# Output projection: high and low activations side by side, 512 columns in one product and 64 in a second

## The chip, the cores and the metric

The kernel runs on one core of a Trainium2 chip. Its time is the device time of one execution in microseconds (us), here the median of the runs shown. The profile of one execution, taken by the hardware, gives the busy time of each engine, every instruction's start and length, and the chain of work that ended last. The engines are TensorE (PE; its weight loads are listed apart as PEld), VectorE (DVE), ScalarE (ACT), GpSimd (POOL) and SyncE (SP), which issues most transfers.

## What is computed

One layer of a decoder for two groups of requests that share their weights: 256 prompt tokens and 8 x 4 sample tokens, 288 tokens together, each of width 4096. The change touches the last matrix product and what follows it:

```
merged = sigmoid(g_a) * (attn @ w_pa) + sigmoid(g_b) * (out_b @ w_pb)
y = merged @ w_o
x = layer_norm(ALPHA * x + gate[:, None] * y, ln_g, ln_b)
```

`w_o` is 4096 x 4096, all data fp32.

## The kernel before

Everything is kept with features on the 128 partitions and the 288 tokens along the row (`T = 288`), so a tile of activations is 128 x 288 and a block of weights 128 x 128. Weights come from memory in units of 128 x 2048 (1 MB, 16 blocks), loaded on SP's queue two units ahead. Each operand is split into a high part (the value cast to fp32r) and a low part (what the cast left out). ScalarE casts half a unit, 8 blocks, to `wH` (line 181), VectorE subtracts to get `wL` (line 182); there are three buffers of either (`HB = 3`). A product of two split operands is then three products in the array, all added up in one PSUM tile (`prod`, lines 190 to 195):

- line 193: `wH` with the high activations,
- line 194: `wH` with the low activations,
- line 195: `wL` with the high activations.

Stages run one after another over one stream of weight units: the modulation and the first column tiles of the input projection (`ada`, `ea`), the other column tiles with attention and gating in the background (`in`), the two merge projections (`p`), and the output projection (`y`). The merge (lines 717 to 743) leaves `merged` split into `mH` and `mL`, two tiles of 16 feature blocks each. The output projection (`o_units`, from line 763) makes 32 tiles of 128 features: 32 blocks of weights for each, in two units, 96 products into one PSUM tile `y` of 128 x 288 out of three such. `post_o` (line 801) then reads `y` from PSUM: the gate is multiplied in and `ALPHA * x` added (lines 805 to 808, VectorE), ScalarE squares (line 815), VectorE adds up sums and squares (lines 820, 821), ScalarE multiplies by the gain (line 824). After the first tile a product with ones (`kp`, line 811) gives a mean that is subtracted from all later tiles. `token_sums` (line 795) sums over features for the norm, and `final` spreads the statistics and writes the result.

Instructions are written in the order of the program and then put in an order for each engine by a scheduler that works with estimates; each engine runs its own list in order. In PSUM there are three tiles with the tag `acc`, four with the tag `bg` for the background work, and one for the modulation.

Of the kernel before, what the change touches and what calls it, by code (L numbers as in the profile page):

```python
# [10 lines left out]
F32 = mybir.dt.float32  # L11
F32R = mybir.dt.float32r
# [6 lines left out]
P = 128  # L19
D = 4096  # L20
KT = D // P
# [52 lines left out]
def first_order(au, eu, extra):  # L74
    """Order of the units of the modulation (au) and of the column tiles summed up as h comes (eu): per unit
    of column tiles, RATIO units of the modulation in the first half of h and RATIO2 in the second, where
    the extra tiles, which need the first half only, fill in. Returns the order and what is left."""
    order = []
    ada = [(c, u) for c, us in enumerate(au) for u in us]
    early = [(c, u) for c, us in enumerate(eu) for u in us]  # L80
    extra = list(extra)
    credit, at, go = 0.0, -1, False
    half = OFFS.index(KT // 2)
    while ada:
        at = ada[0][0]
        ratio = RATIO if at < half else RATIO2
        ready = early and early[0][0] < at
        if ready and at < half and early[0][0] == at - 1 and sum(1 for x in early if x[0] == at - 1) <= RES:
            ready = False
        if credit < 1.0:  # L90
            go = False
        elif credit >= (GE if at < half else GE2):
            go = True
        if go and ready:
            order.append(early.pop(0)[1])
            credit -= 1.0
        elif go and at >= half and extra:
            order.append(extra.pop(0))
            credit -= 1.0
        else:  # L100
            order.append(ada.pop(0)[1])
            credit = min(credit + 1.0 / ratio, CAP + 1.0 / ratio + (GE if at < half else GE2) - 1.0)
    return order, extra[:4] + [u for _, u in early] + extra[4:]
# [6 lines left out]
def build(ctx, tc, nc, I, O):  # L110
# [16 lines left out]

    # constants
    ident = const.tile([P, P], F32, name="ident")
# [16 lines left out]

    # background work: generators stepped between the weight units
    bg = []
# [15 lines left out]

    # weight units
    class Unit:
# [45 lines left out]

# [1 line left out]
    ada_row = [0]  # L214

    # Column group q of the array takes a quarter of the unit's columns; where a chunk has too few of
    # them, groups 0 and 1 take the shift and scale of even rows of weights, 2 and 3 those of odd ones.
    def ada_units(n, fin):
# [100 lines left out]

# [1 line left out]
    Q = slot("Q")  # L321
# [65 lines left out]

# [1 line left out]
    def attn_setup():  # L389
# [51 lines left out]
    def softmax_tail(m, sm, sk, ex, r):  # L441
        # m: the negated maxima; sm: sums without the sink; r: reciprocal of the whole sum
        nc.vector.tensor_tensor(ex, sk, m, ALU.add)
        nc.scalar.activation(ex, ex, AF.Exp)
        nc.vector.tensor_tensor(sm, sm, ex, ALU.add)
        nc.vector.reciprocal(r, sm)

    def attn_group(g):
# [6 lines left out]

        # heads in the order (half, pair), so that each bank is written from one half of the partitions
        def q(half, i, a, b):
            return Q[64 * half:64 * half + 64, 4 * g + i, a:b]
        # scores
        pss = [bgp("s0") for _ in range(2)]  # L460
# [8 lines left out]
        for ih in range(2):  # L469
# [10 lines left out]
            yield 1800  # L480
        # softmax
        st = A["st"].rearrange("p (a n h) -> p a n h", a=4, n=2)
# [14 lines left out]
        for hb in range(2):  # L497
# [5 lines left out]
            yield 1000  # L503
        # sample scores
        Qbd, Qs, Ss = A["Qbd"], A["Qs"], A["Ss"]
        for b in range(NB):
# [4 lines left out]
                                  Q[:, 4 * g:4 * g + 4, NPR + TS * b:NPR + TS * b + TS])  # L511
        # transposes
        for i in range(6):
# [9 lines left out]
        for hf in range(2):  # L523
# [8 lines left out]
            yield 1800  # L532
        # prompt outputs
        for qi in range(4):
# [8 lines left out]
            yield 1300  # L543
        # sample softmax
        m, sm, ex, r = (A["st"][:, 32 + 2 * i:34 + 2 * i] for i in range(4))
# [27 lines left out]

# [1 line left out]
    G = {}  # L575
# [137 lines left out]

# [1 line left out]
    M = {}  # L715

    def p_units(j):
        def load(k):
            t = tmp.tile([P, T], F32, tag="t", name="gl", bufs=6)
            nc.sync.dma_start(t, gdram[32 * k + j])  # L720
            nc.scalar.activation(t, t, AF.Sigmoid)
            return t

        def body_for(name, k):
            def body(u):
                if j == 0 and k == 1:
                    M["H"] = [slot(f"mH{i}", dt=F32R) for i in range(2)]
                    M["L"] = [slot(f"mL{i}", dt=F32R) for i in range(2)]
                t = load(k)
                ps = acc("p")  # L730
                for i in range(16):
                    prod(ps, u, i, G[name + "H"][:, i], G[name + "L"][:, i], i == 0, i == 15)
                nc.vector.tensor_mul(t, t, ps)
                if k == 0:
                    M[j] = t
                else:
                    ta = M.pop(j)
                    nc.vector.tensor_add(t, t, ta)
                    h, lo = M["H"][j // 16][:, j % 16], M["L"][j // 16][:, j % 16]
                    nc.scalar.copy(h, t)  # L740
                    nc.vector.tensor_sub(lo, t, h.bitcast(F32))
            return body
        return [Unit(I["wpa"][j], body_for("A", 0)), Unit(I["wpb"][j], body_for("B", 1))]

# [1 line left out]
    Z = {}  # L746

    def start_final():
        w = slot("fin", (P, 4608))
        cut = lambda i: w[:, P + i * T:P + (i + 1) * T]  # L750
        Z["ones"] = w[:, :P]
        for i, n in enumerate(("K", "s1", "s2", "dg", "dg2", "rstd", "row", "w")):
            Z[n] = cut(i)
        Z["dg"] = w[:, P + 3 * T:P + 5 * T]
        nc.vector.memset(Z["ones"], 1.0)
        nc.vector.memset(Z["row"][0:2], 1.0)
        Z["d"] = [slot(f"d{i}") for i in range(2)]
        Z["gb"] = slot("gb", (P, 4608))[0:2, :D]
        nc.scalar.dma_start(Z["gb"], I["gbrow"])
        # the table of the last square root, ahead of its use  # L760
        nc.scalar.activation(Z["w"][:, 0:1], epst, AF.Sqrt)

    def o_units(j):
        st = {}

        def body_for(half):
            def body(u):
                if half == 0:
                    st["ps"] = acc("y")
                    st["x"] = tmp.tile([P, T], F32, tag="t", name="xl", bufs=6)  # L770
                    nc.sync.dma_start(st["x"], I["xT"][:, j])
                elif j == 0:
                    nc.scalar.mul(st["x"], st["x"], ALPHA)
                else:
                    if j == 1 or j == KT - 1:
                        drain()
                    nc.vector.scalar_tensor_tensor(st["x"], st["x"], ALPHA, Z["K"], ALU.mult, ALU.subtract)
                    if j == KT - 1:
                        Z["st"] = bgp("st")
                        Z["st2"] = bgp("st2")  # L780
                for i in range(16):
                    if half and j == KT - 1 and i == 8:
                        token_sums(Z["s1"], Z["s2"], True)
                    prod(st["ps"], u, i, M["H"][half][:, i], M["L"][half][:, i], half == 0 and i == 0,
                         half == 1 and i == 15)
                if half == 1:
                    post_o(j, st["ps"], st["x"])
            return body
# [11 lines left out]
    def post_o(j, ps, x):  # L800
        # d = ALPHA * x + gate * y - K; K is the mean over the first 128 features, for every token
        z = Z["d"][j // 16][:, j % 16]
# [23 lines left out]
    def final():  # L826
        # the tokens on partitions (3 blocks of TB) for their statistics
        sums = Z["w"][:TB, 18:24]
# [10 lines left out]
        nc.vector.tensor_mul(r2[:, :, 1], mean, r2[:, :, 0])  # L839
        # and spread over all partitions: rstd and -mean * rstd  # L840
        dg = Z["dg"][:TB].rearrange("p (s b t) -> p s b t", s=2, b=3)
# [9 lines left out]

        # out = (d * gain) * rstd + (gain * nmr + bias)
        def tiles(j):
# [23 lines left out]

        # shared out between VectorE and GpSimd; the second term from ScalarE or TensorE
        clock, done = {"g": 0.0, "v": 0.0}, []
# [7 lines left out]

# [1 line left out]
    items = []  # L889
# [127 lines left out]
```

## Time and profile before

| what | value |
|---|---|
| median of two runs (3073.05 and 3073.66) | 3073.36 us |
| span of the profiled execution, first to last instruction | 3070.7 us |
| what the runs shown have beyond that span | 2.7 us by the median (2.3 to 3.0) |
| products of the input projection, `ea` and `in` | 5376 and 8832 |
| products of the merge, `p` | 3072 |
| products of the output projection, `y` | 3072 |
| weight units of the output projection | 64, 1 MB each, 4.9 us from issue to landing |
| first and last product of `y` | at 2630.4 and 3041.5 us |

The profile lists no other time for the profiled execution than its span. "Busy" of TensorE counts a product from its start to its modelled end, and products overlap, so the rate is read from the distance of two starts. In the rows of a group stand the line, the engine, the operation, output and inputs by their names in the program, the tile of the array (rows x columns), the shape, the count, then the busy time, the mean length in ns and the idle time before them.

### The profile page before, as it was taken

The page shows a single profiled execution, that of the slowest core. Times are in us where ns is not written, and L with a number is a line of the kernel's source. Part 1 is how long each engine was busy: PE and PEld are TensorE (multiplying, and loading weights), DVE is VectorE, ACT ScalarE, POOL GpSimd, SP SyncE. Part 2 cuts the span into 40 slices and gives each one's busy share as a digit, 9 for nine tenths or more (in the row PEclk, how much of TensorE's full clock was granted, in tenths as well). Part 3 has the DMA queues.
Part 4 walks back from the last instruction along what each step waited for, and adds up shares of the span by engine and source line. Part 5 has one row for each costly group of instructions (what it writes and reads, how often), then busy time and mean ns, then how long its engine had stood idle before and what let it go on. Part 6 is the DMA issues. An engine that isn't in the chain of part 4 may idle for free.

```text
span 3070.7 us, 53243 instructions
## 1 busy us (share of the span) xinstructions
PE 3036.1 (99%) x23040; PEld 2843.1 (93%) x23040; DVE 1550.5 (50%) x2202; ACT 1080.1 (35%) x1381; POOL 15.4 (1%) x14
## 2 busy tenths in 40 slices
PE   7999999999999999999999999999999999999998
PEld 5888888888999999999999999999999999999997
DVE  3776554444445545445444633444555555555555
ACT  2222223322333434343333333333444444433333
POOL 0000000000000000000000000000000000000001
PEclk8999999999999999999999999999999999999998
DMA  8888877877777565555655565566565555555552
GB/s 333 326 335 327 326 287 297 304 279 285 259 256 262 178 221 209 185 209 205 215 206 206 206 213 200 209 222 215 203 212 188 188 188 188 175 176 177 177 177 95
DMA packets 128383, 700.07 MB, mean 228 GB/s; under 512 B 14802, under 2 KB 44530, under 8 KB 48882
## 3 DMA queue, kind: packets, MB, share of 16 engines
q1 hardware_dynamic: 109440, 669.56, 60.8%
q10 hardware_dynamic: 18708, 27.10, 2.5%
q8 instruction: 181, 2.97, 0.4%
q14 instruction: 54, 0.44, 0.0%
HBM read 676.85 MB, written 19.46 MB: 227 GB/s over the span
## 4 chain that ended last, share of the span: by engine, by line
PE 98%; DMA 1%; DVE 1%; issue 0%; ACT 0%; ACTq 0%; DVEq 0%; SPq 0%
PE in L193 13%; PE in L195 13%; PE in L194 13%; PE ea L193 8%; PE ea L194 8%; PE ea L195 8%; PE ada L233 6%; PE p L193 5%; PE y L193 5%; PE p L195 4%; PE y L195 4%; PE p L194 4%; PE y L194 4%; DMA lngb<-lngb 0%; DMA raw<-wada 0%; PE pT L517 0%
## 5 line engine op out<-in xcount | busy, mean ns | idle before, releaser
L181 ACT CAST wH<-raw 128x1024 fp32r<-128x1024 f32 x848 | 888.8, 1050 | 1841.5 <-PE in L194 813.1
L182 DVE TENSOR_TENSOR wL<-raw,wH 128x1024 fp32r<-128x1024 f32 x848 | 1035.4, 1224 | 973.6 <-ACT wH L181 970.8
L193 PE MATMUL in<-hH,wH 128*128 128x288 f32 x2944 | 883.1, 300 | 0.0
L194 PE MATMUL in<-hL,wH 128*128 128x288 f32 x2944 | 870.5, 296 | 0.0
L195 PE MATMUL in<-hH,wL 128*128 128x288 f32 x2944 | 866.7, 294 | 0.0
L193 PEld LDWEIGHTS in<-hH,wH 128*128 128x128 f32 x2944 | 552.2, 188 | 32.7 <-ACT wH L181 9.2
L195 PEld LDWEIGHTS in<-hH,wL 128*128 128x128 f32 x2944 | 554.7, 188 | 0.0
L194 PEld LDWEIGHTS in<-hL,wH 128*128 128x128 f32 x2944 | 553.1, 188 | 0.1
L193 PE MATMUL ea<-hH,wH 128*128 128x288 f32 x1792 | 537.3, 301 | 2.4 <-ACT hH L297 2.4
L194 PE MATMUL ea<-hL,wH 128*128 128x288 f32 x1792 | 529.8, 296 | 1.4 <-DVE hL L298 1.4
L195 PE MATMUL ea<-hH,wL 128*128 128x288 f32 x1792 | 524.7, 295 | 0.0
L193 PEld LDWEIGHTS ea<-hH,wH 128*128 128x128 f32 x1792 | 336.7, 188 | 52.4 <-ACT wH L181 23.9
L194 PEld LDWEIGHTS ea<-hL,wH 128*128 128x128 f32 x1792 | 337.7, 188 | 1.9 <-DVE hL L298 1.8
L195 PEld LDWEIGHTS ea<-hH,wL 128*128 128x128 f32 x1792 | 337.3, 189 | 1.7 <-issue 0.8
L193 PE MATMUL y<-mH,wH 128*128 128x288 f32 x1024 | 303.4, 296 | 0.0
L194 PE MATMUL y<-mL,wH 128*128 128x288 f32 x1024 | 302.6, 296 | 0.0
L195 PE MATMUL y<-mH,wL 128*128 128x288 f32 x1024 | 301.4, 294 | 0.0
L233 PE MATMUL ada<-raw,cT 128*32 128x512 f32 (+1 forms) x1792 | 202.0, 549 | 16.2 <-ACT cT L136 8.2
L195 PEld LDWEIGHTS y<-mH,wL 128*128 128x128 f32 x1024 | 193.1, 189 | 0.1
L194 PEld LDWEIGHTS y<-mL,wH 128*128 128x128 f32 x1024 | 192.4, 188 | 0.1
L193 PEld LDWEIGHTS y<-mH,wH 128*128 128x128 f32 x1024 | 192.1, 188 | 0.0
L193 PE MATMUL p<-AH,wH 128*128 128x288 f32 x512 | 151.8, 297 | 0.0
(200 smaller groups left out, 2388.7 us busy)
## 6 DMA issues: line engine op xcount, KB each, us to landing
raw<-wada SPq DMA_DIRECT2D x192, 1024.0 KB, 5.2
raw<-wr SPq DMA_DIRECT2D x184, 1024.0 KB, 5.1
raw<-we SPq DMA_DIRECT2D x112, 1024.0 KB, 7.2
raw<-wo SPq DMA_DIRECT2D x64, 1024.0 KB, 4.9
raw<-wpa SPq DMA_DIRECT2D x32, 1024.0 KB, 4.9
raw<-wpb SPq DMA_DIRECT2D x32, 1024.0 KB, 4.9
gl<-gdram SPq DMA_DIRECT2D x64, 144.0 KB, 3.2
pdram<-part ACTq DMA_DIRECT2D x32, 144.0 KB, 4.6
```

What stands on the lines that cost most here:

```text
L181: nc.scalar.copy(h, s)
L182: nc.vector.tensor_sub(lo, s, h.bitcast(F32))
L193: mm(ps, wh, xh, start=first, stop=False)
L194: mm(ps, wh, xl, start=False, stop=False)
L195: mm(ps, wl, xh, start=False, stop=last)
L233: mm(st["ps"][32 * q:32 * q + 32, :w], cT[:, kt, :], u.raw[:, at:at + w], start=kt < 1 + paired, stop=kt >= KT - 1 - paired)
```

## The change

The merge now writes the high and low part of a feature block side by side: four tiles `mHL` of 8 feature blocks, each block 2 x 288 columns. The output projection passes these 576 columns by `wH` in two products, the first 512 and the last 64, into two PSUM tiles; `wL` with the 288 high columns is the third and adds to the first 288 columns of the wide tile. At the end of an output tile the two halves of the sum are put together in SBUF, and `post_o` reads that. The second PSUM tile has the tag `bg`. Nothing else of the program is changed.

```
-                    M["H"] = [slot(f"mH{i}", dt=F32R) for i in range(2)]
-                    M["L"] = [slot(f"mL{i}", dt=F32R) for i in range(2)]
+                    M["HL"] = [slot(f"mHL{i}", (P, 8, 2, T), F32R) for i in range(4)]
...
-                    h, lo = M["H"][j // 16][:, j % 16], M["L"][j // 16][:, j % 16]
+                    h, lo = M["HL"][j // 8][:, j % 8, 0], M["HL"][j // 8][:, j % 8, 1]
...
+    WIDE = 512
+
+    def prod_wide(ps, ps2, unit, m, hl, first, last):
+        pump(PUMP)
+        wh, wl = unit.block(m)
+        flat = hl.rearrange("p s t -> p (s t)")
+        mm(ps, wh, flat[:, :WIDE], start=first, stop=False)
+        mm(ps2[:, :2 * T - WIDE], wh, flat[:, WIDE:], start=first, stop=last)
+        mm(ps[:, :T], wl, hl[:, 0], start=False, stop=last)
...
-                    st["ps"] = acc("y")
+                    st["ps"] = ps_acc.tile([P, WIDE], F32, tag="acc", name="y")
+                    st["ps2"] = bgp("y2")
...
-                    prod(st["ps"], u, i, M["H"][half][:, i], M["L"][half][:, i], half == 0 and i == 0,
-                         half == 1 and i == 15)
+                    k = half * 16 + i
+                    prod_wide(st["ps"], st["ps2"], u, i, M["HL"][k // 8][:, k % 8], k == 0, k == KT - 1)
                 if half == 1:
-                    post_o(j, st["ps"], st["x"])
+                    y = tmp.tile([P, T], F32, tag="t", name="ysum", bufs=6)
+                    n = WIDE - T
+                    nc.scalar.copy(y, st["ps"][:, :T])
+                    nc.vector.tensor_add(y[:, :n], y[:, :n], st["ps"][:, T:])
+                    nc.vector.tensor_add(y[:, n:], y[:, n:], st["ps2"][:, :T - n])
+                    post_o(j, y, st["x"])
```

What this does to the order of the engines' lists. TensorE, end of the first output tile and start of the second, before (the numbers after the names tell buffers apart):

```order
L193 MATMUL y_25537<-mH1_21524,wH_25459 128x288
L194 MATMUL y_25537<-mL1_21526,wH_25459 128x288
L195 MATMUL y_25537<-mH1_21524,wL_25460 128x288
L193 MATMUL y_25670<-mH0_21523,wH_25529 128x288
L194 MATMUL y_25670<-mL0_21525,wH_25529 128x288
L195 MATMUL y_25670<-mH0_21523,wL_25530 128x288
```

And now, with the wide product on line 770, the narrow one on 771 and the third on 772:

```order
L770 MATMUL y_25537<-mHL3_21526,wH_25459 128x512
L771 MATMUL y2_25538<-mHL3_21526,wH_25459 128x64
L772 MATMUL y_25537<-mHL3_21526,wL_25460 128x288
L770 MATMUL y_25675<-mHL0_21523,wH_25529 128x512
L772 MATMUL y_25675<-mHL0_21523,wL_25530 128x288
```

Three products a block as before, of other widths; in the second tile alone the narrow products of the first ten blocks are put off. They follow the product `kp`, which before stood two blocks and a product into the tile:

```order
L195 MATMUL y_25670<-mH0_21523,wL_25530 128x288
L193 MATMUL y_25670<-mH0_21523,wH_25529 128x288
L811 MATMUL kp_25651<-d0_25522,fin_25519 128x288
L194 MATMUL y_25670<-mL0_21525,wH_25529 128x288
L195 MATMUL y_25670<-mH0_21523,wL_25530 128x288
```

TensorE at the same place now, ten blocks into the tile:

```order
L770 MATMUL y_25675<-mHL1_21524,wH_25533 128x512
L772 MATMUL y_25675<-mHL1_21524,wL_25534 128x288
L828 MATMUL kp_25656<-d0_25522,fin_25519 128x288
L771 MATMUL y2_25676<-mHL0_21523,wH_25529 128x64 x8
L771 MATMUL y2_25676<-mHL1_21524,wH_25533 128x64 x2
```

The mean of the first tile is taken eight blocks later than before. From the third tile on the three products of every block stand together.

VectorE at the end of a tile in the middle of the stage, before:

```order
L805 TENSOR_TENSOR t2_26812<-y_26702,gate_82 128x32
L808 SCALAR_TENSOR_TENSOR d0_25522<-y_26702,gate_82,xl_26703 128x256
L807 TENSOR_TENSOR d0_25522<-t2_26812,xl_26703 128x32
L820 TENSOR_TENSOR fin_25519<-fin_25519,d0_25522 128x288
L182 TENSOR_TENSOR wL_26756<-raw_26753,wH_26755 128x1024
L821 TENSOR_TENSOR fin_25519<-fin_25519,sq_26816 128x288
```

VectorE at the same place now:

```order
L802 TENSOR_TENSOR ysum_26858<-ysum_26858,y_26747 128x224
L803 TENSOR_TENSOR ysum_26858<-ysum_26858,y2_26748 128x64
L822 TENSOR_TENSOR t2_26862<-ysum_26858,gate_82 128x32
L825 SCALAR_TENSOR_TENSOR d0_25522<-ysum_26858,gate_82,xl_26749 128x256
L824 TENSOR_TENSOR d0_25522<-t2_26862,xl_26749 128x32
L837 TENSOR_TENSOR fin_25519<-fin_25519,d0_25522 128x288
L838 TENSOR_TENSOR fin_25519<-fin_25519,sq_26866 128x288
L182 TENSOR_TENSOR wL_26806<-raw_26799,wH_26805 128x1024
```

Two adds have come in ahead, and the next `wL` stands behind the sum of squares instead of ahead of it. ScalarE there, before:

```order
L181 CAST wH_26755<-raw_26753 128x1024
L815 ACTIVATE sq_26816<-d0_25522 128x288
L824 ACTIVATE d0_25522<-d0_25522,lngb_81 128x288
L181 CAST wH_26759<-raw_26753 128x1024
L181 CAST wH_26823<-raw_26821 128x1024
```

ScalarE now:

```order
L181 CAST wH_26801<-raw_26799 128x1024
L801 COPY ysum_26858<-y_26747 128x288
L832 ACTIVATE sq_26866<-d0_25522 128x288
L181 CAST wH_26805<-raw_26799 128x1024
L841 ACTIVATE d0_25522<-d0_25522,lngb_81 128x288
L181 CAST wH_26873<-raw_26871 128x1024
```

The copy from PSUM has come in ahead of the square, and the multiplication by the gain stands one cast later.

## The prediction

> **What bounds the kernel now.** I read the page first (shares of the engines, the chain that ended last), then the output projection by windows, then single products.
>
> ```profile
> span 3070.7 us, 53243 instructions
> PE 3036.1 (99%) x23040; PEld 2843.1 (93%) x23040; DVE 1550.5 (50%) x2202; ACT 1080.1 (35%) x1381; POOL 15.4 (1%) x14
> ...
> PE 98%; DMA 1%; DVE 1%; issue 0%; ACT 0%; ACTq 0%; DVEq 0%; SPq 0%
> ```
>
> TensorE holds 98% of the chain. No other engine is above 50% busy, so a nanosecond more or less per product is a nanosecond of the end, times the number of products. The stage in question, by windows (engine busy time and number of instructions, then the granted clock):
>
> ```profile
> core 0: us, PE busy (x) PEld busy (x) DVE busy (x) ACT busy (x) POOL busy (x), PEclk, DMA share, GB/s
> 2650.00:3030.00 380.00, 380.00 (x2852) 380.00 (x2852) 198.37 (x298) 151.47 (x179) 0.00 (x0) 1.00 0.49 167
> ```
>
> 380.00 us for 2852 products are **133.2 ns for a product of 288 columns**, some 400 ns for the three of a weight block, at a granted clock of 1.00; the 32 x 32 = 1024 blocks of the stage take 410 us. The busy time of one product (296 ns in the next row) is longer than that because products overlap; the distance of two starts is what counts.
>
> ```profile
> L193 PE MATMUL y<-mH,wH 128*128 128x288 f32 x951 | 281.8, 296 | 0.0
> ...
> L182 DVE TENSOR_TENSOR wL<-raw,wH 128x1024 fp32r<-128x1024 f32 x119 | 145.6, 1223 | 149.8 <-ACT wH L181 149.8
> L181 ACT CAST wH<-raw 128x1024 fp32r<-128x1024 f32 x119 | 125.1, 1052 | 228.7 <-PE y L194 228.7
> ```
>
> The products wait for nothing (0.0), ScalarE waits for TensorE (228.7 us), VectorE for ScalarE: TensorE sets the pace. Each product has a weight load of its own, also where the weights are the same as in the product before (the loads of lines 193 and 194 are both `wH`). A load starts with the product before its own:
>
> ```profile
> 2643.72 0.29 PE L194 MATMUL y<-mL,wH 128*128 128x288 f32 x1
> 2643.72 0.19 PEld L195 LDWEIGHTS y<-mH,wL 128*128 128x128 f32 x1
> 2643.85 0.29 PE L195 MATMUL y<-mH,wL 128*128 128x288 f32 x1
> 2643.85 0.19 PEld L193 LDWEIGHTS y<-mH,wH 128*128 128x128 f32 x1
> ```
>
> At 2643.72 the product of line 194 starts, and in the same hundredth the load for line 195, whose product starts at 2643.85. So one load is under way at a time, behind one running product. A product can therefore start no sooner than one load time after the product before it. How long is that? Where the columns are few, the load must show. Lines 517 and 795 have such products (one row of the timeline each, then the mean of one):
>
> ```profile
> 1075.95 0.60 PE L517 MATMUL pT<-ident,attP 128*128 128x128 f32 x4
> ...
> L517 PE MATMUL pT<-ident,attP 128*128 128x128 f32 x96 | 14.4, 272 | 0.0
> ...
> 3037.43 1.10 PE L795 MATMUL st<-fin 128*96 128x1 f32 x12
> ...
> L795 PE MATMUL st<-fin 128*96 128x1 f32 x12 | 1.1, 218 | 0.0
> ...
> 101.05 0.19 PEld L193 LDWEIGHTS ea<-hH,wH 128*128 128x128 f32 x1 [0.41 <-issue]
> 101.16 0.19 PEld L194 LDWEIGHTS ea<-hL,wH 128*128 128x128 f32 x1
> ```
>
> Four products of 128 columns: (0.60 - 0.272) / 3 = 0.109 us from start to start. Twelve products of a single column, with 96 columns of weights: (1.10 - 0.218) / 11 = 0.080 us, 0.84 ns for each column of weights, so 107 ns for 128. And the first two loads after a pause stand 0.11 us apart. **Three rows give 107 to 110 ns as the least distance of two products with 128 columns of weights**, however few columns they pass. The 288-column products hide it, with 133 - 109 = 24 ns to spare.
>
> By the Trainium skill, "TensorE: Matmul & The Clock Gate", section "LDWEIGHTS (loading the stationary operand)", a load takes its number of weight columns divided by 1.2 ns, whatever the rows; that is 106.7 ns here, and the sum below would be 2 us lower by it. This is the rule that speaks against the change, and the three rows bear it out.
>
> **The change, part by part.** It keeps the number of products (three a block, 3072) and of columns passed: 3 x 288 = 864 = 512 + 64 + 288. So if a product cost its columns alone, nothing would change. Only the way the 864 are cut differs.
>
> *The wide product (W), start to start.* No row has 512 columns in this form. Upper end: all of the 133.3 ns is by the column, 512 / 288 x 133.3 = 237. Lower end: what the columns cost in the other form, in which a product is run twice over and a quarter of the array works on each:
>
> ```profile
> 368.21 1.92 PE L233 MATMUL ada<-raw,cT 128*32 128x512 f32 x16
> ...
> L233 PE MATMUL ada<-raw,cT 128*32 128x512 f32 x1280 | 163.3, 599 | 0.0
> ```
>
> Sixteen, four at a time: (1.92 - 0.599) / 3 = 0.440 us for 512 columns. The 288-column products pass 1.86 times as many columns per ns (288 / 133.3 against 512 / 440). If that is really a factor of 2 with a fixed part in each product, 512 columns cost 220 ns and the fixed part, which is 133.3 - 288 x 0.43 = 9.5; without the fixed part, 220. The four rows of a round don't start quite together, so 220 may be up to 3% too much (213). I take 228, the middle of 220 and 237.
>
> *The narrow product (S), from its start to that of the third.* Its 64 columns would take 64 x 133.3 / 288 = 30 ns; that is the lower end, if its load or the next one were hidden. But the load of the third product's `wL` can start only with the narrow product, and takes 107 to 110. I take 109, the row of 128 columns, which is the nearest. Upper end inside this case: 120, if so short a product passes its columns at the rate of the other form, twice over (2 x 64 x 0.86 = 110, plus the 9.5).
>
> *The third product* is one of 288 columns as before: 133.3.
>
> Sum: 228 + 109 + 133.3 = 470 ns a block against 400; +70.3 x 1024 = **+72.0 us**.
>
> *The end of a tile* (32 times). One ScalarE copy from PSUM and two VectorE adds come in; the later steps read SBUF.
>
> ```profile
> L609 ACT COPY t<-in 128x288 f32<-128x288 f32 x16 | 6.3, 391 | 0.0
> ...
> L808 DVE SCALAR_TENSOR_TENSOR d<-y,gate,xl 128x256 f32<-128x256 f32 x30 | 14.2, 475 | 0.0
> ...
> L805 DVE TENSOR_TENSOR t<-y,gate 128x32 f32<-128x32 f32 x30 | 5.7, 191 | 30.8 <-PE y L195 30.8
> ```
>
> Copy 0.39 us; adds of 224 and 64 elements between 0.19 and 0.475, say 0.43 and 0.2. 32 x 0.39 = 12.5 us of ScalarE and 32 x 0.63 = 20 us of VectorE go into idle times of 228.7 and 149.8 us. What stands behind the new wait: ScalarE's copy waits for the tile's last product, and behind it stand the square and the casts of the next weights; VectorE's adds wait for the copy. A tile has four groups of eight blocks, and there are three buffers for groups. From the tile's end E by the order: cast of the next tile's third group (1.05) E+1.1, its `wL` (1.22) E+2.3, adds E+3.0, the gate steps (0.19, 0.475, 0.18) E+3.8, square and sums E+4.7, cast of its fourth group (free when the first is used up) E+4.9, its `wL` E+6.1. TensorE needs that one 24 blocks after E, at 24 x 0.47 = 11.3 us. Five microseconds of cover; without them the products would wait for `wL`. I cost it at nothing. Not hidden is the last tile, where everything follows its last product: 0.39 + 0.63 and two hand-overs, +1.1 us. At the first tile the product of line 828 (`kp`) needs the first finished row, at about E+3.8, and the order puts ten blocks without their narrow products ahead of it (10 x 0.36 = 3.6 us): +0.3 us at most. The narrow products held back there cost the same 109 each.
>
> *Queues.* SP issues the same 64 weight loads and 32 loads of `xl` in the same order, POOL is unchanged. The stage moves the same bytes in a longer time.
>
> Sum of all: 72.0 + 1.1 + 0.3 = 73.4 us on a span of 3070.7. The median of the two runs, 3073.4, lies 2.7 above that span, and I add the same to it: **3147 us**.
>
> **The rivals.**
>
> *The wide product at its floor* (chance 0.12): W is 213 to 216, S 107 to 109, so the block is 453 to 458 and the time 3129 to 3135. For it: the rate of the other form. Against it: the 288-column products don't reach that rate (133.3 against 124). By the skill's same page, section "Back-to-back issue gap", a product costs its columns divided by 2.4 plus 2.5 ns; that would be 215.8 for 512 and a time of 3134. The same rule gives 122.5 for 288 columns, where the trace has 133.2, so it holds here only in part.
>
> *Not slower: the narrow product needs no load of its own or its successor's is ready* (0.09). Then S is about 30 to 40 ns, the block 228 + 40 + 133 = 401, and the time 3073 + 1 + 1.4 = 3075. It decides if S is under 97 (there the block is 458.7, 2% slower). For it: the weights are those of the product before. Against it: line 194 has its own load for weights that line 193 just used, and a load never starts ahead of the product before it.
>
> *Not slower: the pace is by the product, not by the column* (0.05). If 133 ns are what any product takes up to some width, W is 133 too, and the block 133 + 109 + 133 = 375: 1024 x -25 = -26, 3049 us. It decides if W is below 158 (block 400). For it: every stage shows the same 133 ns. Against it: line 517's products stand 109 apart, not 133. The skill's section "Back-to-back issue gap" names some 131 ns a product as sustained at 512 columns, which would give nearly this; no run here shows it.
>
> *The narrow product is run twice over* (0.07), as those of plain fp32 are (the six products that one call of line 795 makes are the twelve quoted above). Two loads: S = 218, block 579, +184 us, 3258 us. Against it: the operand type is the same as in the products of 288 columns, which run once.
>
> **How the numbers follow.** Forecast 0.66, wide at the floor 0.12, no load 0.09, by the product 0.05, twice over 0.07; 0.01 is left for a gain over 2%. Two per cent (61 us, a time of 3135) is about what a measurement of this kernel can tell from no change. Slower: 0.66 + 0.07 = 0.73. Within 2%: 0.12 + 0.09 + 0.05 = 0.26. Faster: 0.01. The range: low end W 213, S 107, block 453.3, +54.6 + 1 = 3129, so 3130; high end W 237, S 120, block 490.3, +92.5 + 1.4 = 3167, so 3170. The two first cases lie in it, 0.78; the others are too far off to reach.
>
> **What would show it.** Distances of starts in the stage: wide to narrow 220 to 237 ns, narrow to third 107 to 120, third to wide 133; the load of line 772 starting with the narrow product; 3072 products in the stage as before; TensorE without idle time for `wL` or `wH`. I am wrong if the narrow product has no load row, if its load starts during the wide product together with that of `wL`, if the narrow product appears twice, or if products wait for VectorE or ScalarE in the middle of the stage.

## The result, and the profile after

| | before | changed |
|---|---|---|
| median | 3073.36 us (2 runs) | 3148.24 us (2 runs, 3147.82 and 3148.67) |
| span of the profiled execution | 3070.7 us | 3146.0 us |

The ratio is 1.0246, with a 95% interval from 1.0229 to 1.0263: slower by 74.9 us. The forecast was 3147.

The page of the changed kernel, shares of the engines and the chain that ended last:

```profile
PE 3111.7 (99%) x23040; PEld 2874.8 (91%) x23040; DVE 1569.2 (50%) x2266; ACT 1085.9 (35%) x1413; POOL 15.4 (0%) x14
...
PE 98%; DMA 1%; DVE 1%; issue 0%; ACT 0%; ACTq 0%; DVEq 0%; SPq 0%
```

TensorE is still the whole chain, with the same 23040 products. Its weight loads fell from 93% of the span to 91%: something now keeps them from running back to back. A stretch in the middle of the output projection, by windows (columns as in the prediction's windows; the counts in brackets are products and weight loads):

```profile
2660.00:3050.00 390.00, 390.00 (x2474) 354.99 (x2473) 188.77 (x311) 136.11 (x181) 0.00 (x0) 1.00 0.44 150
```

390.00 us for 2474 products, three a block, are **472.9 ns a block**; before it was 380.00 / 2852 x 3 = 399.7. The difference of 73.2 ns, times 1024 blocks, is 75.0 us: the whole loss lies in the pace of the blocks. The granted clock is 1.00 in both. Now the groups of that stage (the last number is the idle time before them):

```profile
L770 PE MATMUL y<-mHL,wH 128*128 128x512 f32 x930 | 364.7, 392 | 0.0
L772 PE MATMUL y<-mHL,wL 128*128 128x288 f32 x931 | 350.1, 376 | 0.0
L771 PE MATMUL y<-mHL,wH 128*128 128x64 f32 x930 | 178.4, 192 | 0.0
...
L772 PEld LDWEIGHTS y<-mHL,wL 128*128 128x128 f32 x930 | 174.3, 187 | 39.5
```

The same product before the change:

```profile
L195 PE MATMUL y<-mH,wL 128*128 128x288 f32 x950 | 279.6, 294 | 0.0
```

No product waits for another engine. But the third product, 288 columns as ever, has a mean of 376 ns instead of 294, and the loads stood idle for 39.5 us ahead of the load for line 772. The timeline of one block shows both:

```profile
2800.00 0.39 PE L770 MATMUL y<-mHL,wH 128*128 128x512 f32 x1
2800.00 0.19 PEld L771 LDWEIGHTS y<-mHL,wH 128*128 128x128 f32 x1
...
2800.23 0.19 PE L771 MATMUL y<-mHL,wH 128*128 128x64 f32 x1
2800.23 0.19 PEld L772 LDWEIGHTS y<-mHL,wL 128*128 128x128 f32 x1
2800.26 0.38 PE L772 MATMUL y<-mHL,wL 128*128 128x288 f32 x1
2800.34 0.19 PEld L770 LDWEIGHTS y<-mHL,wH 128*128 128x128 f32 x1
2800.47 0.39 PE L770 MATMUL y<-mHL,wH 128*128 128x512 f32 x1
```

The load for line 772 starts at 2800.23, with the narrow product. The third product's row begins 0.03 us later, about the time that 64 columns take at the rate of the others, but it is 0.08 us too long: as we read it, it stands there without its weights. The next load should start with the third product, as loads do in the prediction's lines; it comes only at 2800.34, 0.11 us after the load before it. So a block is 0.23 (wide), 0.11 (one load, with the narrow product inside it) and 0.13 (third).

At the end of the last tile, from the start of the last product to the first product of the norm:

```profile
3115.60 0.38 PE L772 MATMUL y<-mHL,wL 128*128 128x288 f32 x1
...
3117.64 0.33 PE L812 MATMUL st<-fin,d 128*96 128x1 f32 x2 [1.66 <-DVE d L825]
```

TensorE stands idle for 1.66 us there. The row at the same place in the trace of before:

```profile
3042.50 0.33 PE L795 MATMUL st<-fin,d 128*96 128x1 f32 x2 [0.68 <-DVE d L808]
```

There it was 0.68 us, so the copy and the adds cost 1.0 us, once.

### The profile page after: what moved, and what is told of

The parts are those of the page before. It is cut to its first block, busy times and chain, and to the rows that moved or that the text cites. A ratio compares the mean times of both kernels' runs of the same rounds, so it can differ in the third digit from the quotient of the medians.

```text
span 3146.0 us, 53341 instructions
## 1 busy us (share of the span) xinstructions
PE 3111.7 (99%) x23040; PEld 2874.8 (91%) x23040; DVE 1569.2 (50%) x2266; ACT 1085.9 (35%) x1413; POOL 15.4 (0%) x14
## 4 chain that ended last, share of the span: by engine, by line
PE 98%; DMA 1%; DVE 1%; issue 0%; ACT 0%; ACTq 0%; DVEq 0%; SPq 0%
PE in L193 13%; PE in L195 12%; PE in L194 12%; PE ea L193 8%; PE ea L194 8%; PE ea L195 8%; PE y L770 7%; PE y L772 7%; PE ada L233 6%; PE p L193 4%; PE p L195 4%; PE p L194 4%; PE y L771 1%; DMA lngb<-lngb 0%; DMA raw<-wada 0%; PE pT L517 0%
## 5 line engine op out<-in xcount | busy, mean ns | idle before, releaser
L770 PE MATMUL y<-mHL,wH 128*128 128x512 f32 x1024 | 401.5, 392 | 0.0
L772 PE MATMUL y<-mHL,wL 128*128 128x288 f32 x1024 | 384.2, 375 | 0.0
L772 PEld LDWEIGHTS y<-mHL,wL 128*128 128x128 f32 x1024 | 191.9, 187 | 43.1
L771 PE MATMUL y<-mHL,wH 128*128 128x64 f32 x1024 | 196.0, 193 | 0.0
L770 PEld LDWEIGHTS y<-mHL,wH 128*128 128x128 f32 x1024 | 195.0, 190 | 0.4
L771 PEld LDWEIGHTS y<-mHL,wH 128*128 128x128 f32 x1024 | 192.3, 188 | 0.1
```

The costliest lines, as they stand in the source:

```text
L770: mm(ps, wh, flat[:, :WIDE], start=first, stop=False)
L771: mm(ps2[:, :2 * T - WIDE], wh, flat[:, WIDE:], start=first, stop=last)
L772: mm(ps[:, :T], wl, hl[:, 0], start=False, stop=last)
```

## The experiments

The theory: a product starts no sooner after the one before than its own weight load takes (109 ns for 128 columns of weights), and else it costs its columns. The rivals: the loss lies in the layout, the second PSUM tile or the work at the end of a tile; or a product with few columns passes them slowly, so that the 110 ns are those of the 64 columns themselves; or the wide product is what costs.

**Other cuts of the 576 columns.** The edit is one number; the wide PSUM tile is still made with 512 columns, of which the first `WIDE` are used, and for 288 the add of zero columns goes:

```
-    WIDE = 512
+    WIDE = 288
```

> The 576 columns are cut 288 and 288 instead of 512 and 64; the side-by-side layout, the second PSUM tile, the copy and one add of 288 at a tile's end stay. Load theory (a product starts no sooner than 109 ns after the one before, the time of its own weight load, and else takes its columns): three products of 133 ns, block 400, stage as before, 1.5 us more at the end: 3075 us. Rival, the loss lies in the layout, the second PSUM tile or the work at a tile's end: about 3148 us, as changed.

Measured 3070.34 us, ratio to before 0.9993 (0.9984 to 1.0002). The whole loss is gone, with the layout, the second tile, the copy and one add at the tile's end still there. The rival that puts it in those is out.

```
-    WIDE = 512
+    WIDE = 384
```

> Cut 384 and 192. Load theory, with a wide product of 7.3 ns + 0.437 ns a column (a line through 133.3 at 288 and 231 at 512): 175 + 109 + 133 = 417 ns a block, 3092 us. Rival, a product of fewer than 256 columns passes them slowly (the 110 ns of 64 columns would be 1.7 ns a column): 192 columns take 330, block 638, 3319 us.

Measured 3092.35 us, ratio 1.0065 (1.0048 to 1.0082).

```
-    WIDE = 512
+    WIDE = 448
```

> Cut 448 and 128. Load theory: 203 + 109 + 133 = 445 ns a block, 3121 us. Rival, short products pass their columns slowly: 128 columns take 220, block 556, 3234 us.

Measured 3121.16 us, ratio 1.0157 (1.0142 to 1.0173).

```
-    WIDE = 512
+    WIDE = 336
```

> Cut 336 and 240. Load theory: the narrow product's own columns, 7.3 + 0.437 x 240 = 112 ns, are as long as a load; 154 + 112 + 133 = 399 ns a block, as before the change: 3075 us. Rival, products under 256 columns pass them slowly (1.7 ns each): 240 take 412, block 699, 3381 us.

Measured 3071.36 us, ratio 0.9996 (0.9987 to 1.0005). The windows of cut 384, of cut 448 and of cut 336:

```profile
2660.00:3030.00 370.00, 370.00 (x2655) 370.00 (x2654) 202.00 (x334) 148.70 (x194) 0.00 (x0) 1.00 0.48 166
```

```profile
2660.00:3050.00 390.00, 390.00 (x2622) 376.72 (x2621) 200.54 (x332) 146.55 (x194) 0.00 (x0) 1.00 0.46 159
```

```profile
2680.00:3020.00 340.00, 340.00 (x2567) 340.00 (x2566) 196.43 (x323) 143.65 (x188) 0.00 (x0) 1.00 0.50 171
```

370.00 / 2655 x 3 = 418.1 ns and 390.00 / 2622 x 3 = 446.2 ns a block, against 417 and 445 expected, and 472.9 at 512. Each 64 columns moved from the short product to the wide one cost 27 to 28 ns, while the short one gets no cheaper: on the mean of over 800 blocks, the load behind that of line 772 starts 108 ns after it at 192, 128 and 64 columns alike. At 240 columns the short product is as long as a load and nothing is lost against the kernel before (340.00 / 2567 x 3 = 397.4 ns). Were short products slow by the column, 240 of them would have been the worst case. The timeline of cut 336 shows the balance:

```profile
2800.42 0.27 PE L771 MATMUL y<-mHL,wH 128*128 128x240 f32 x1
2800.42 0.19 PEld L772 LDWEIGHTS y<-mHL,wL 128*128 128x128 f32 x1
2800.53 0.30 PE L772 MATMUL y<-mHL,wL 128*128 128x288 f32 x1
2800.53 0.19 PEld L770 LDWEIGHTS y<-mHL,wH 128*128 128x128 f32 x1
```

Here the third product has its ordinary 0.30 us, and it starts together with the next load, so its weights were there when the 240 columns were through.

**Without the narrow product**, so that the last 64 tokens lose one of the three parts of the sum:

```
-        mm(ps2[:, :2 * T - WIDE], wh, flat[:, WIDE:], start=first, stop=last)
...
-                    nc.vector.tensor_add(y[:, n:], y[:, n:], st["ps2"][:, :T - n])
```

> The product of 64 columns is left out, and with it the add that takes it up: the last 64 tokens lose their high-weight by low-activation part. Load theory: the block is 231 + 133 = 364 ns, 36 less than before the change: 3037 us, 111 below the changed kernel. If the 64 columns cost only their share of columns (30 ns), the loss of the change lies in the wide product and leaving the narrow one out gives 3148 - 31 = 3117 us.

Measured 3036.02 us, ratio 0.9881 (0.9866 to 0.9896).

```profile
2660.00:2960.00 300.00, 300.00 (x1653) 263.60 (x1652) 180.51 (x284) 138.35 (x180) 0.00 (x0) 1.00 0.55 195
```

Two products a block: 300.00 / 1653 x 2 = 363.0 ns. So the narrow product costs 472.9 - 363.0 = 109.9 ns, though at the rate of the others its 64 columns would be some 30. The wide and the third product together cost 363, 7 ns less than their 800 columns would at the rate of before (800 / 288 x 133.2 = 370), so the wide product is not where the loss lies.

**A narrow product of 16 columns** (48 tokens lose the same part):

```
-        mm(ps2[:, :2 * T - WIDE], wh, flat[:, WIDE:], start=first, stop=last)
+        mm(ps2[:, :16], wh, flat[:, WIDE:WIDE + 16], start=first, stop=last)
```

> The narrow product passes 16 columns instead of 64 (48 tokens lose their high-weight by low-activation part). Load theory: its 109 ns are a load time and stay: 3148 us. Rival, its 110 ns are 64 slow columns (1.7 ns each): 16 columns take 28, the next load no more than that, block 391: 3064 us. If columns count at the usual 0.44 ns, 21 ns less a block: 3127 us.

Measured 3151.32 us (3149.9 to 3152.73), ratio 1.0256 (1.0239 to 1.0273).

```profile
2660.00:3050.00 390.00, 390.00 (x2463) 353.55 (x2462) 182.16 (x311) 137.98 (x181) 0.00 (x0) 1.00 0.43 148
```

390.00 / 2463 x 3 = 475.0 ns a block. A quarter of the columns buys nothing, and both rivals, 3064 and 3127, are out. In these two traces the block is even 2 ns longer than with 64 columns, which the theory does not give; the intervals of the two ratios overlap. From load to load (means again), the 2 ns stand in the wide product, 232.8 against 230.8; the load that decides takes 108.3 in both.

**Fewer columns of weights in the third product.** In all blocks but the last of a tile `wL` is loaded with 96 of its 128 columns (a quarter of the output features loses most of its third part):

```
-        mm(ps[:, :T], wl, hl[:, 0], start=False, stop=last)
+        c = P if last else 96
+        mm(ps[:c, :T], wl[:, :c], hl[:, 0], start=False, stop=last)
```

> The third product takes 96 of the 128 columns of wL as weights in every block but the last of a tile (32 of 128 output features lose most of their low-weight part); all three products pass as many columns as in the changed kernel. Load theory: the distance from the narrow to the third product is the load of the third's weights, 84 ns for 96 columns (line 795's distance) instead of 109: 25 less a block, 3148 - 26 = 3122 us. Rival, the narrow product itself takes 110 ns, or its own load does: 3148 us, no change.

Measured 3122.15 us, ratio 1.0162 (1.0147 to 1.0177). All three products pass the columns that they passed before, and the narrow one has the same load as ever; only the load behind it is shorter. Window and timeline (line 773 is the third product here):

```profile
2660.00:3050.00 390.00, 390.00 (x2617) 352.47 (x2616) 200.33 (x332) 143.27 (x192) 0.00 (x0) 1.00 0.46 159
```

```profile
2800.42 0.19 PE L771 MATMUL y<-mHL,wH 128*128 128x64 f32 x1
2800.42 0.16 PEld L773 LDWEIGHTS y<-mHL,wL 128*96 128x96 f32 x1
2800.45 0.35 PE L773 MATMUL y<-mHL,wL 128*96 128x288 f32 x1
2800.50 0.19 PEld L770 LDWEIGHTS y<-mHL,wH 128*128 128x128 f32 x1
```

390.00 / 2617 x 3 = 447.1 ns a block, 25.8 less than the changed kernel's 472.9; the next load now comes 0.08 us after the narrow product's start instead of 0.11. This settles which load it is: that of the product behind the narrow one. The 84 ns expected is near what ten of the eleven distances of line 795's products have when they are read one by one, 85 ns; the prediction's 80 is the mean of all eleven, and the first is only 27. By the Trainium skill, "TensorE: Matmul & The Clock Gate", section "LDWEIGHTS (loading the stationary operand)", the load's time goes with its columns of weights; by its figure, as an estimate, 128 and 96 of them differ by 26.7 ns, and the 25.8 measured here agree with it.

**Layout and second tile apart.** The window of cut 288:

```profile
2680.00:3020.00 340.00, 340.00 (x2573) 340.00 (x2573) 192.13 (x297) 144.04 (x188) 0.00 (x0) 1.00 0.50 171
```

It ran its block in 340.00 / 2573 x 3 = 396.4 ns, three less than the kernel before. Two kernels take its two differences one at a time. The layout alone:

```
-        mm(ps, wh, flat[:, :WIDE], start=first, stop=False)
-        mm(ps2[:, :2 * T - WIDE], wh, flat[:, WIDE:], start=first, stop=last)
-        mm(ps[:, :T], wl, hl[:, 0], start=False, stop=last)
+        mm(ps, wh, flat[:, :T], start=first, stop=False)
+        mm(ps, wh, flat[:, T:], start=False, stop=False)
+        mm(ps, wl, flat[:, :T], start=False, stop=last)
...
-                    post_o(j, y, st["x"])
+                    post_o(j, st["ps"], st["x"])
```

> The side-by-side layout alone: three products of 288 columns into one PSUM tile, the end of a tile as before the change. Cut 288/288 ran its block in 396.4 ns against 399.7 before. If the layout does that, the block is 396.4 here too and the time 3070 us; if it is the second PSUM tile or chance, 399.7 and 3073 us.

Measured 3069.07 us, ratio 0.9989 (0.9980 to 0.9998). The second tile alone, put into the kernel before:

```
-        mm(ps, wh, xl, start=False, stop=False)
+        if ps2 is None:
+            mm(ps, wh, xl, start=False, stop=False)
+        else:
+            mm(ps2, wh, xl, start=first, stop=last)
...
+                    y = tmp.tile([P, T], F32, tag="t", name="ysum", bufs=6)
+                    nc.scalar.copy(y, st["ps"])
+                    nc.vector.tensor_add(y, y, st["ps2"])
+                    post_o(j, y, st["x"])
```

> The second PSUM tile alone: the layout of before (high and low parts in tiles of their own), the product with the low activations into a second PSUM tile, copy and add at a tile's end. If the second tile makes the block 396.4 ns, 3071 us; if the layout does, 399.7 ns and 3074.5 us, the end being 1.5 us longer.

Measured 3074.26 us, ratio 1.0005 (0.9996 to 1.0014). The same window of the two, the layout first:

```profile
2680.00:3020.00 340.00, 340.00 (x2574) 340.00 (x2573) 179.82 (x270) 136.04 (x161) 0.00 (x0) 1.00 0.49 171
```

```profile
2680.00:3020.00 340.00, 340.00 (x2552) 340.00 (x2552) 190.18 (x294) 142.83 (x187) 0.00 (x0) 1.00 0.49 170
```

396.3 ns with the layout, 399.7 with the second tile, which is the pace of before. The layout does it, and with it alone the kernel has the lowest median of all that compute the whole sum, a tenth of a per cent below before; its interval overlaps those of cuts 288 and 336.

## Why the prediction was right

- *The floor of one load.* This was the term that decided, and it held: 109 ns taken, 109.9 measured by leaving the narrow product out, 108.3 from load to load. The ten narrow products held back in the second tile stand in a row there, eight of their nine distances 112 ns. That the load is the cause is shown by the run with 96 columns of weights; the rival of slow short products is ruled out by the cuts and by 16 columns.
- *Where the 109 came from.* Here there was luck: the row of line 517, from which it was taken, can't tell a load from columns. Its 128 columns would take 110 ns at the rate of line 233's form, too, and line 557's product, a transpose like it, keeps the same distance to a product with only 32 columns of weights:

```profile
1139.91 0.27 PE L557 MATMUL sT<-ident,attT 128*128 128x128 f32 x1
1140.02 0.27 PE L558 MATMUL sT<-ident,attT 128*32 128x128 f32 x1
```

- *The other two rows for it.* Of line 795 the distances are 85 ns and not 80 (see the run with 96 columns of weights), which in proportion makes 113 for 128 columns and not 107. The pair of loads after a pause, 0.11 us apart, is the row that bears the term out.
- *One load at a time.* The lines shown for it don't show that: a load's row is 0.19 us long, and the next load starts after 0.13. What the runs bound is the distance of two loads' starts; how long one load lasts stays open.
- *The wide product.* 228 taken, between 220 and 237. From its start to the narrow product's it is 231 ns on the mean in the changed kernel. From 384 to 512 columns the block grows by 54.8 ns, 0.428 ns a column, which leaves about 231 - 512 x 0.428 = 12 ns for a fixed part. So neither end was right: the cost is by the column with a fixed part, as the middle assumed, and the fixed part was put at 9.5. This is the term that the sum had too low, by 3 ns; the rival with the wide product at 213 to 216 is out. The estimate of 215.8 ns for 512 columns by the Trainium skill, "TensorE: Matmul & The Clock Gate", section "Back-to-back issue gap", is too low here by some 15 ns.
- *The third product.* 133 taken, 134 from load to load; the sum 470 against a measured 472.9.
- *The end of a tile.* Costed at nothing in the middle and at 1.1 us for the last tile; no product waited (0.0), and the last tile cost 1.0. Cut 288 carries nearly the same work and shows no loss.
- *What would show it.* The load of line 772 does start with the narrow product, and wide to narrow is 0.23 us. But the narrow-to-third distance of 107 to 120 does not stand in the rows of the products: the third's row starts after 0.03 us and is longer instead. The distance has to be read from the loads, where it is 0.11.
- *What the sum left out.* That the layout by itself gains some 3 ns a block was not foreseen. With the layout alone 2.2 of them stand between the third product and the next block's first: 131.0 ns against 133.2 before, on the mean. Without the narrow product that distance is 131.3; in the changed kernel, from load to load, it is 134, so there this part of the gain does not show.
- *The rivals.* A narrow product without a load, a pace by the product and a product run twice are all excluded by the after trace: its load rows number as many as before, wide to narrow is 231, and there is one row of line 771 a block.

The steps add up: from the first product of `y` to the last it is 411.2 us before and 486.1 now, 74.9 more; behind the last product it is 1.3 more, of which 1.0 is the wait shown above; and the stage starts 0.8 sooner. Together that is 75.4, the difference of the spans (75.3 by the rounded figures above).

## What to carry to other kernels

Count weight loads as well as columns. Where each product brings its own weights, as in this kernel, a product costs the longer of its columns and the load of the product behind it. With 128 columns of weights a product of fewer than some 230 columns of this kind wastes the difference (an estimate: 12 ns and 0.428 a column reach 109.9 there; 240 columns lost nothing, 192 did). Cutting a row of columns unevenly, to fill one product to the brim, is worth nothing if it leaves a remnant that a load does not fit behind. The two cuts whose parts all take at least a load's time, 288 with 288 and 336 with 240, cost nearly the same: 396.4 and 397.4 ns a block.

## What had not been expected of the hardware

The high and low activations side by side, in the same order of products and with the same columns, ran a block in 396.3 ns instead of 399.7 (3069.07 us, ratio 0.9989, 0.9980 to 0.9998). The two traces have the same number of products, and in neither does a product of the stage wait for another engine. Whether it is the place of the tiles or their form that does it is open: no run moved the tiles without changing their layout. Also open is why the wide product takes 2 ns longer ahead of 16 columns than ahead of 64, if it is more than chance.
